# Gather operations and splits of weights ordered behind each hand-over's chain on VectorE, and a gather that pauses

## The chip, the cores and the metric

The kernel runs on one core of one Trainium2 chip, launched once. The metric is device time in microseconds: 3865.21 us, the median of three runs of the kernel before (3860.94 to 3874.12). TensorE (PE), VectorE (DVE), ScalarE (ACT), GpSimd (POOL) and SyncE (SP) run their own instruction streams in order; transfers are issued from SP's and POOL's queues.

## The reference

The input is 256 tokens of 1024 numbers, a memory and a context of 256 rows each, and a conditioning vector, all in fp32. Two blocks stand one after the other; cut to what matters:

```python
for l in range(2):                                       # first block
    x = x + 0.5 * rms_norm(swiglu(rms_norm(x, ng[0]), w_gu[l, 0], w_down[l, 0]), ng[1])   # ffn l0
    h = rms_norm(x, ng[2])
    tok, qm = retention_mixer(h, ...) if l == 0 else mla_mixer(h, ...)
    mix = concatenate([tok, memory_attention(qm, mem_n, w_kv[l])]) @ w_o[l]
    x = x + rms_norm(mix, ng[3])
    x = x + 0.5 * rms_norm(swiglu(rms_norm(x, ng[4]), w_gu[l, 1], w_down[l, 1]), ng[5])   # ffn l1
```

The second block takes that x as its latents, and a context of its own. Its scales, shifts and gates are the product of silu(c) with a large matrix (the modulation). Its even layer mixes latents and context (an mLSTM and a differential attention), its odd layer has a windowed attention; a PEER feed-forward follows each. PEER scores 128 by 128 expert keys, picks 16 experts for each of 8 heads, and computes

```python
eidx, gate = top-k picks                                  # 128 experts for each token
a = einsum('nd,nhkd->nhk', xt, u[eidx])                   # a dot product with each picked row of u
y = einsum('nhk,nhkd->nd', gate * gelu(a), v[eidx])       # a weighted sum of the picked rows of v
```

## The kernel before

Activations of 256 tokens stay in SBUF as two token tiles of 128. Weights stream in through transfers (`raw`). Every fp32 weight is split into a high part that ScalarE casts (L253, `wh`) and the rest, `wl`, that VectorE or GpSimd subtracts (L260); a product is then three matmuls (L370 to L372). Which of the two engines subtracts is counted out by a share; VectorE is the default.

Two streams are generated in turn and put in order by priority. The main one is the chain of layers: memory, ffn00, retention, ffn01, ffn10, mla, ffn11, the even layer of the latents, PEER, the odd layer, PEER. The side one computes the modulation, the context's even layer, and the context's PEER by a pick and a gather: scores and top-k (L1468 to L1600, on VectorE), and then for each of two token tiles 128 indirect transfers of rows of `u` (512 KB each, `pg`, L1636, on GpSimd) with a dot product each on VectorE (L311), and 128 of rows of `v` with a weighted sum (L1667). The rows land in a small ring of buffers: a transfer waits until the dot that read its buffer has run. These operations keep their program order among themselves ("pinned", L313).

The rest of the modulation (`mod1`) runs along with the gather: after every third pair of gather operations, once `nalong` has reached `MS`, the generator takes a step (L1614). A step issues weights on GpSimd's queue into a ring of `RN` = 4 buffers, and has TensorE multiply them (L912, `ps<-raw,cT`).

Where one layer ends and the next begins there is a hand-over: `post_add` multiplies the layer's result by its gain (L482) and takes its sum of squares; `rsqrt` computes a reciprocal root in small operations on 128 numbers (L281, L282, and three times L286 and L290); L486 adds to x; the next norm takes its sum of squares (L298 on ScalarE, L304, L306) and root in the same way and multiplies (L343, and L345 where there is a shift); TensorE transposes (L318), and L264 and L265 split the result into `xh` and `xl`. Only then can TensorE begin the next layer.

Of the kernel before, what the change touches and what calls it, by code (L numbers as in the profile page):

```python
# [8 lines left out]
F32 = mybir.dt.float32  # L9
# [157 lines left out]
class Kern:  # L167
# [3 lines left out]
    def __init__(s, ctx, tc, nc, d):  # L171
        s.ctx, s.tc, s.nc, s.d = ctx, tc, nc, d
        P = lambda n, b, **k: ctx.enter_context(tc.tile_pool(name=n, bufs=b, **k))
        s.cp = P("cst", 1)
        s.rawp = P("raw", NR)
        s.rings = {"m": (s.rawp, P("hl", NH), NR, NH, 1024, NL)}
        s.stream = "m"
        s.xtp = P("xt", 1)
        s.rp = P("res", 1)
        s.bcp = P("bc", 2)  # L180
        s.smp = P("small", 4)
        s.psp = P("ps", 1, space=PSUM)
        s.dramp = P("dram", 1, space=bass.MemoryType.DRAM)
        s.n = 0
        s.nsplit = 0
        s.share = s.base = DS
        s.cst = {}
        s.consts("base", s.cp)
        s.junk = s.cp.tile([128, 512], BF16, name="junk")
        s.ident = s.c("ident")  # L190
        s.mod, s.R = {}, {}
        s.owed = s.before = s.square = None
        s.nalong = 0

    def dq(s, out, in_):

# [51 lines left out]
    def split(s, src, n=1024):  # L248

        nc = s.nc  # L250
        ring = s.rings.get(s.stream) or s.rings["m"]
        hi = ring[1].tile([128, ring[4]], F32R, tag="wh", name=s.nm("wh"), bufs=ring[3])[:, :n]
        nc.scalar.copy(hi, src)  # L253
        s.nsplit += s.share[0]
        eng = nc.vector
        if s.nsplit >= s.share[1]:
            s.nsplit -= s.share[1]
            eng = nc.gpsimd
        lo = ring[1].tile([128, ring[4]], F32R, tag="wl", name=s.nm("wl"), bufs=ring[5])[:, :n]
        eng.tensor_tensor(lo, src, hi.bitcast(F32), op=OP.subtract)  # L260
        return hi, lo

    def split_to(s, hi, lo, src):
# [12 lines left out]
    def rsqrt(s, xh, n, tag="rs"):  # L276
# [1 line left out]
        nc = s.nc  # L278
        y = s.sm([128, n], tag + "y", I32)
        a = s.sm([128, n], tag + "a")  # L280
        nc.vector.tensor_scalar(y, xh.bitcast(I32), 1, None, op0=OP.arith_shift_right)  # L281
        nc.vector.tensor_scalar(y, y, -1.0, float(0x5F3759DF - 2 ** 31 - 2 ** 22), op0=OP.mult, op1=OP.add)  # L282
        yf = y.bitcast(F32)
        for _ in range(3):
            if n == 1:
# [23 lines left out]
    def dot(s, a, b, out):  # L309

        return s.nc.vector.scalar_tensor_tensor(a, a, 1.0, b, op0=OP.mult, op1=OP.mult, accum_out=out)  # L311

    def pin(s, i):  # L313
        return s.tc.keep_in_program_order(i) if s.pinned else i

    def tr(s, dst, src):
# [22 lines left out]
    def norm_tok(s, xn, x, mul, add, out=None):  # L339
        nc = s.nc  # L340
        halves = lambda a: [a[:, i * 512:i * 512 + 512].rearrange("p (a b) -> p a b", a=4) for i in range(2)]
        r = s.rstd(halves(x), halves(xn) if out is None else out, D)
        nc.vector.scalar_tensor_tensor(xn, x, r, mul, op0=OP.mult, op1=OP.mult)  # L343
        if add is not None:
            nc.vector.tensor_tensor(xn, xn, add, op=OP.add)  # L345

    @contextmanager
    def ahead(s, by):
# [6 lines left out]
    def norm_T(s, x, mul, add=None, kind="w", side=None, xT=None, xf=None):  # L355
        xT = xT or s.xt_tiles()
        with s.pool("np", side) as pl, s.ahead(AH):
            xn = [pl.tile([128, D], F32, tag=f"xn{t}", name=s.nm("xn")) for t in range(2)]
            rest = s.settle(xn)
            for t in range(2):  # L360
                rest(t)
                s.norm_tok(xn[t], x[:, t], mul, add)
                s.transpose_split(xn[t], xT, t, kind, xf)
        return xT


# [901 lines left out]
    def even(s, ep, x, l, v, C, kind, tk, side):  # L1268
# [4 lines left out]
        with s.pool("evo", side) as po:  # L1273
# [20 lines left out]
            with s.pool("evn", side) as pl, s.ahead(AH if lat else 0):  # L1294
# [3 lines left out]
                for t in range(2):  # L1298
# [5 lines left out]
                        s.dq(xi, x[t])  # L1304
                    s.norm_tok(xo, xi, rows[0], rows[1])
                    s.transpose_split(xo, xT, t, tk)
            with s.pool("evi", side) as pl:
                yield from s.even_in(pl, E, xT, lat, C, R, kind, tk)
            xp.close()
# [315 lines left out]
    def gather(s, hc, l, v, side, also):  # L1625
# [5 lines left out]
        with s.pool("pgg", side) as op, s.psum("psg") as pg:  # L1631
# [17 lines left out]
            for t in range(2):  # L1649
# [5 lines left out]
                for k, gt in rows(t, "u0"):  # L1655
                    s.pin(s.dot(gt, xm, A[:, k:k + 1]))
                    if k % 2:
                        yield s.gcost + s.along(also)
                nc.scalar.activation(A, A, AF.Gelu)
                nc.vector.tensor_tensor(A, A, gates[t], op=OP.mult)  # L1660
                y = pg.tile([128, D], F32, tag="pxy", name=s.nm("py"))
# [251 lines left out]
FS = (1, 1)  # L1913
FN = 2
A0 = (1, 4)
AH = 15
ME = 3
MS = 12
DB = 2
DS = (1, 4)  # L1920
OFF = dict(mod1=0, cev=0, croute=0, pick=200, gather=200)
# [58 lines left out]
```

## Time and profile before

| | |
|---|---|
| median of three runs | 3865.21 us (3860.94 to 3874.12) |
| the profiled execution | 3871.0 us |
| its span, first to last instruction | 3869.2 us |
| mean granted TensorE clock | 0.925 |
| busy: TensorE / VectorE / ScalarE / GpSimd | 3420.9 / 2706.3 / 1567.9 / 1366.4 us |
| transfers, mean over the span | 242 GB/s |

Busy times are of one execution, and shares of the whole span hide that stages have different limits; a stretch's own row tells which engine is full there. An engine's idle time is put down to what came last before the waiting instruction. The engines execute in order, so an instruction that waits holds all that stands behind it on its engine.

### The profile page before, as it was taken

How to read it: one execution, taken by the hardware profiler on the slowest of the kernel's cores; microseconds unless marked ns; L12 is line 12 of the kernel's file. 1: busy time of each engine (PE TensorE's matmuls, PEld its weight loads, DVE VectorE, ACT ScalarE, POOL GpSimd, SP SyncE). 2: the span in 40 equal slices, each digit the busy share in tenths (PEclk: the TensorE clock that was granted, in tenths of full speed). 3: DMA queues.
4: the chain of work that ended last, by engine and by line, in shares of the span. 5: the costliest groups of instructions: out<-in, count | busy, mean ns of one | idle time of the engine just before them, and what ended most of it. 6: DMA issues, size and time to landing. Idle time of an engine off the chain costs nothing.

```text
span 3869.2 us, 55141 instructions
## 1 busy us (share of the span) xinstructions
PE 3420.9 (88%) x20576; PEld 2943.2 (76%) x20576; DVE 2706.3 (70%) x5107; ACT 1567.9 (41%) x2435; POOL 1366.4 (35%) x1012
## 2 busy tenths in 40 slices
PE   5998966889899789798798799999978999899998
PEld 3776855678788578676687688889755889899987
DVE  5456788776666667787899777878976629754444
ACT  3454423343443534343213344444445115444444
POOL 3333325145445245430325366666710000122121
PEclk7999978889899889885899899999989999999999
DMA  7456549569788468761779899999941457876664
GB/s 279 145 169 216 185 161 364 185 242 327 254 314 313 169 220 298 285 232 63 255 248 387 293 339 353 352 329 341 390 126 45 142 164 248 275 243 209 196 193 150
DMA packets 316557, 938.13 MB, mean 242 GB/s; under 512 B 34608, under 2 KB 99552, under 8 KB 312192
## 3 DMA queue, kind: packets, MB, share of 16 engines
q1 hardware_dynamic: 216912, 578.25, 44.3%
q0 software_dynamic: 99376, 356.35, 25.5%
q8 instruction: 162, 2.65, 0.3%
q14 instruction: 107, 0.88, 0.1%
HBM read 894.80 MB, written 39.68 MB: 242 GB/s over the span
## 4 chain that ended last, share of the span: by engine, by line
PE 56%; DVE 17%; issue 10%; DMA 7%; POOL 7%; ACT 3%; POOLq 0%; SPq 0%; ACTq 0%; DVEq 0%
PE ps L370 14%; PE ps L371 14%; PE ps L372 14%; PE ps L417 6%; POOL pg L1636 3%; POOL wl L260 3%; DVE wl L260 2%; DVE pg L311 2%; PE ps L318 2%; DVE py L1667 1%; DMA raw<-in_modw 1%; DMA raw<-in_ffn 1%; ACT wh L253 1%; PE ps L1700 1%; DMA raw<-in_ut 1%
## 5 line engine op out<-in xcount | busy, mean ns | idle before, releaser
L253 ACT CAST wh<-raw 128x1024 fp32r<-128x1024 f32 (+3 forms) x927 | 918.6, 992 | 1062.5 <-PE ps L372 725.3
L260 DVE TENSOR_TENSOR wl<-raw,wh 128x1024 fp32r<-128x1024 f32 (+3 forms) x653 | 781.8, 1201 | 492.2 <-ACT wh L253 485.2
L260 POOL TENSOR_TENSOR wl<-raw,wh 128x1024 fp32r<-128x1024 f32 (+2 forms) x274 | 623.6, 2277 | 1397.8 <-ACT wh L253 1225.8
L370 PE MATMUL ps<-xh,wl 128*128 128x256 f32 x3008 | 872.4, 290 | 49.4 <-DVE wl L260 23.0
L371 PE MATMUL ps<-xl,wh 128*128 128x256 f32 x3008 | 864.7, 288 | 0.0
L372 PE MATMUL ps<-xh,wh 128*128 128x256 f32 x3008 | 864.4, 288 | 0.0
L370 PEld LDWEIGHTS ps<-xh,wl 128*128 128x128 f32 x3008 | 590.1, 196 | 75.7 <-DVE wl L260 26.5
L371 PEld LDWEIGHTS ps<-xl,wh 128*128 128x128 f32 x3008 | 590.2, 196 | 7.1 <-issue 2.0
L372 PEld LDWEIGHTS ps<-xh,wh 128*128 128x128 f32 x3008 | 589.5, 196 | 3.6 <-issue 3.1
L1636 POOL DMA_INDIRECT pg<-in_u,eidx x256 | 313.3, 1224 | 405.9 <-DVE pg L311 305.0
L1636 POOL DMA_INDIRECT pg<-in_v,eidx x256 | 306.5, 1197 | 398.6 <-DVE py L1667 189.6
L371 PE MATMUL ps<-wl,Wh 128*128 128x512 f32 x1024 | 403.6, 394 | 11.5 <-DVE wl L260 6.3
L370 PE MATMUL ps<-wh,Wl 128*128 128x512 f32 x1024 | 402.0, 393 | 6.5 <-DVE Wl L265 6.5
L372 PE MATMUL ps<-wh,Wh 128*128 128x512 f32 x1024 | 400.5, 391 | 0.0
L417 PE MATMUL ps<-xf,raw 128*128 128x256 f32 x1664 | 370.7, 384 | 2.3 <-ACT xf L337 2.3
L417 PEld LDWEIGHTS ps<-xf,raw 128*128 128x128 f32 x1664 | 318.4, 193 | 46.3 <-ACT xf L337 3.1
L1667 DVE SCALAR_TENSOR_TENSOR py<-pg,pA,py 128x1024 f32<-128x1024 f32 x254 | 325.9, 1283 | 7.0 <-DMA pg<-in_v,eidx 3.5
L311 DVE SCALAR_TENSOR_TENSOR pg<-pg,pxm 128x1024 f32<-128x1024 f32 x256 | 304.5, 1214 | 14.6 <-ACT pxm L1653 8.1
L371 PE MATMUL ps<-wl,xh 128*128 128x512 f32 (+4 forms) x656 | 254.0, 387 | 15.3 <-POOL wl L260 11.2
L370 PE MATMUL ps<-wh,xl 128*128 128x512 f32 (+4 forms) x656 | 247.6, 385 | 7.3 <-DVE xl L265 4.4
L372 PE MATMUL ps<-wh,xh 128*128 128x512 f32 (+4 forms) x656 | 248.5, 379 | 0.0
L371 PEld LDWEIGHTS ps<-wl,Wh 128*128 128x128 f32 x1024 | 193.8, 189 | 56.5 <-DVE wl L260 9.7
(488 smaller groups left out, 4791.7 us busy)
## 6 DMA issues: line engine op xcount, KB each, us to landing
raw<-in_ffn SPq DMA_DIRECT2D x264, 512.0 KB
raw<-in_ut SPq DMA_DIRECT2D x256, 512.0 KB
raw<-in_v SPq DMA_DIRECT2D x256, 512.0 KB
raw<-in_modw POOLq DMA_DIRECT2D x96, 512.0 KB
Gd<-Gst SPq DMA_DIRECT2D x32, 1024.0 KB
Gq<-Gd SPq DMA_DIRECT2D x30, 1024.0 KB
raw<-in_wq SPq DMA_DIRECT2D x32, 512.0 KB
raw<-in_evin POOLq DMA_DIRECT2D x24, 512.0 KB
```

Of the source, the lines that this page charges most:

```text
L253: nc.scalar.copy(hi, src)
L260: eng.tensor_tensor(lo, src, hi.bitcast(F32), op=OP.subtract)
L311: return s.nc.vector.scalar_tensor_tensor(a, a, 1.0, b, op0=OP.mult, op1=OP.mult, accum_out=out)
L318: s.nc.tensor.transpose(dst, src, s.ident[:src.shape[0], :src.shape[0]])
L370: mm(out, a[1], b[0], start=start, stop=False)
L371: mm(out, a[0], b[1], start=False, stop=False)
L372: mm(out, a[0], b[0], start=False, stop=stop)
L417: s.nc.tensor.matmul(out, src[:, k * 128:(k + 1) * 128], xf[:, k], start=(k == 0), stop=(k == 7))
L1636: nc.gpsimd.indirect_dma_start(out=got[i], out_offset=None, in_=d[tab], in_offset=bass.IndirectOffsetOnAxis(ap=eidx[t][:, k:k + 1], axis=0))
L1667: s.pin(nc.vector.scalar_tensor_tensor(y, gt, wk, y, op0=OP.mult, op1=OP.add))
L1700: nc.tensor.matmul(pb[:, t * 128:(t + 1) * 128], M[:, k, :, t0 + t], OJ[:, (t0 + t) // 2, :, t % 2], start=(k == 0), stop=(k == 1))
```

## The change

- `split`: in the main stream the first three splits (`HU`) after each hand-over put their `wl` on VectorE, whatever the share says; the second and third are ordered behind the last instruction of the norm.
- `rsqrt`: the shift and the multiply-add on the integer become one operation.
- `norm_tok`: the product with the gain (and the shift's addition) is done in two halves of 512 columns.
- `handed` and `pin`: the first pinned gather operation that is generated after a hand-over is ordered behind the last instruction of that norm. Both orderings are on the same engine and need no semaphore.
- `gather`: after the first 12 dots have been generated, the generator yields without work until three hand-overs (memory, ffn00 and retention) have been generated.
- `MS` goes from 12 to 7.

```diff
@@ split
+        hand = s.stream == "m" and s.hand
         if s.nsplit >= s.share[1]:
             s.nsplit -= s.share[1]
-            eng = nc.gpsimd
+            eng = eng if hand else nc.gpsimd
...
-        eng.tensor_tensor(lo, src, hi.bitcast(F32), op=OP.subtract)
+        i = eng.tensor_tensor(lo, src, hi.bitcast(F32), op=OP.subtract)
+        if hand:
+            if s.hand < HU:
+                s.after(i, s.last_m)
+            s.hand -= 1
@@ rsqrt
-        nc.vector.tensor_scalar(y, xh.bitcast(I32), 1, None, op0=OP.arith_shift_right)
-        nc.vector.tensor_scalar(y, y, -1.0, float(0x5F3759DF - 2 ** 31 - 2 ** 22), op0=OP.mult, op1=OP.add)
+        nc.vector.tensor_scalar(y, xh.bitcast(I32), -0.5, float(0x5F3759DF - 2 ** 31 - 2 ** 22), op0=OP.mult, op1=OP.add)
@@ new, and pin
+    def after(s, i, j):
+        s.tc.add_manual_dep(i.ins, j.ins.name, mybir.DependencyInfo(
+            mybir.DependencyClass.NoSync, mybir.DependencyReason.DATA), reason="behind the hand-over")
+    def handed(s):
+        s.held = s.last_m = s.last
+        s.hand = HU
+        s.nhands += 1
     def pin(s, i):
+        if s.held is not None:
+            s.after(i, s.held)
+            s.held = None
         return s.tc.keep_in_program_order(i) if s.pinned else i
@@ norm_tok
-        nc.vector.scalar_tensor_tensor(xn, x, r, mul, op0=OP.mult, op1=OP.mult)
-        if add is not None:
-            nc.vector.tensor_tensor(xn, xn, add, op=OP.add)
+        for i in range(2):
+            h = slice(i * 512, i * 512 + 512)
+            s.last = nc.vector.scalar_tensor_tensor(xn[:, h], x[:, h], r, mul[:, h], op0=OP.mult, op1=OP.mult)
+            if add is not None:
+                s.last = nc.vector.tensor_tensor(xn[:, h], xn[:, h], add[:, h], op=OP.add)
@@ norm_T, at its end (and in even, for the latents)
+            if s.stream == "m":
+                s.handed()
@@ gather, behind every second dot
+                    if t == 0 and k == 2 * GW - 1:
+                        while s.nhands < 3:
+                            yield None
@@ constants
+HU = 3
+GW = 6
-MS = 12
+MS = 7
```

In the after listings line numbers are shifted: L394 to L396 are L370 to L372 of before, L936 is L912, L317 is L311, L365 is L343, L272 is L265, L296 and L292 are L290 and L286, L1662 is L1636, and L200 is L198.

First place: TensorE in the tail of ffn00, where the down projection's matmuls (`ps<-wh,hh`) change over to the next unit of the up projection (`ps<-xh,wl`). Before:

```order
L371 MATMUL ps_1316<-wl_5204,hh_5019 128x512
L372 MATMUL ps_1316<-wh_5202,hh_5019 128x512
L371 MATMUL ps_1317<-wl_5204,hh_5019 128x512
L372 MATMUL ps_1317<-wh_5202,hh_5019 128x512
L912 MATMUL ps_5123<-raw_4174,cT_289 32x256
L370 MATMUL ps_5145<-xh_1242,wl_5148 128x256
L371 MATMUL ps_5145<-xl_1243,wh_5146 128x256
L372 MATMUL ps_5145<-xh_1242,wh_5146 128x256
```

The same place of TensorE in the changed order:

```order
L395 MATMUL ps_1319<-wl_5062,hh_4907 128x512
L396 MATMUL ps_1319<-wh_5060,hh_4907 128x512
L394 MATMUL ps_1316<-wh_5148,hlo_4996 128x512
L394 MATMUL ps_1317<-wh_5148,hlo_4996 128x512
L394 MATMUL ps_1318<-wh_5148,hlo_4996 128x512
L394 MATMUL ps_1319<-wh_5148,hlo_4996 128x512
L394 MATMUL ps_5091<-xh_1244,wl_5094 128x256
L395 MATMUL ps_5091<-xl_1245,wh_5092 128x256
L396 MATMUL ps_5091<-xh_1244,wh_5092 128x256
```

The matmul of the modulation (L912 on `raw_4174`) stood between the two; it now comes first in the retention.

Second place: VectorE in the hand-over from ffn00 to the retention, around the norm's product (`xn<-x,sm,bc`) of both token tiles; `pg` are the gather's dots. Before:

```order
L343 SCALAR_TENSOR_TENSOR xn_5569<-x,sm_5615,bc_5562 128x1024
L290 SCALAR_TENSOR_TENSOR sm_5648<-sm_5649,sm_5648 128x1
L311 SCALAR_TENSOR_TENSOR pg_5315,pA_4190<-pg_5315,pxm_4188 128x1024
L286 TENSOR_SCALAR sm_5649<-sm_5648,sm_5645 128x1
L311 SCALAR_TENSOR_TENSOR pg_5318,pA_4190<-pg_5318,pxm_4188 128x1024
L265 TENSOR_TENSOR xl_5565<-ps_5626,xh_5564 128x4x128
L265 TENSOR_TENSOR xl_5565<-ps_5633,xh_5564 128x4x128
L290 SCALAR_TENSOR_TENSOR sm_5648<-sm_5649,sm_5648 128x1
L311 SCALAR_TENSOR_TENSOR pg_5325,pA_4190<-pg_5325,pxm_4188 128x1024
L286 TENSOR_SCALAR sm_5649<-sm_5648,sm_5645 128x1
L311 SCALAR_TENSOR_TENSOR pg_5328,pA_4190<-pg_5328,pxm_4188 128x1024
L290 SCALAR_TENSOR_TENSOR sm_5648<-sm_5649,sm_5648 128x1
```

The same place of VectorE in the changed order, from the first product on:

```order
L365 SCALAR_TENSOR_TENSOR xn_5471<-x,sm_5515,bc_5464 128x512 x2
L292 TENSOR_SCALAR sm_5549<-sm_5548,sm_5545 128x1
L296 SCALAR_TENSOR_TENSOR sm_5548<-sm_5549,sm_5548 128x1
L292 TENSOR_SCALAR sm_5549<-sm_5548,sm_5545 128x1
L296 SCALAR_TENSOR_TENSOR sm_5548<-sm_5549,sm_5548 128x1
L365 SCALAR_TENSOR_TENSOR xn_5472<-x,sm_5548,bc_5464 128x512
L272 TENSOR_TENSOR xl_5467<-ps_5526,xh_5466 128x4x128
L272 TENSOR_TENSOR xl_5467<-ps_5533,xh_5466 128x4x128
L365 SCALAR_TENSOR_TENSOR xn_5472<-x,sm_5548,bc_5464 128x512
L263 TENSOR_TENSOR wl_5597<-raw_5589,wh_5595 128x768
L272 TENSOR_TENSOR xl_5467<-ps_5559,xh_5466 128x4x128
L272 TENSOR_TENSOR xl_5467<-ps_5566,xh_5466 128x4x128
```

The dots that stood between the norm's operations are gone from this place; the first of them stands behind the norm and five splits, and 34 more than before stand between this norm and ffn01's hand-over. The pick's last operations, which stood ahead of the dots, now stand between this hand-over's first operations, two of L1558 and two of L1559 among them.

Third place: GpSimd in the retention, `raw` the modulation's weights and `pg` the gathers. Before:

```order
L1636 DMA pg_5523<-in_u,eidx_2878 128x1024
L1636 DMA pg_5526<-in_u,eidx_2878 128x1024
L198 DMA raw_5730<-in_modw 128x1024
L1636 DMA pg_5723<-in_u,eidx_2878 128x1024
L1636 DMA pg_5726<-in_u,eidx_2878 128x1024
L198 DMA raw_5736<-in_modw 128x1024
L198 DMA modg_6181<-in_n12r 4x256
L1636 DMA pg_5819<-in_u,eidx_2878 128x1024
L1636 DMA pg_5822<-in_u,eidx_2878 128x1024
```

GpSimd in the retention in the changed order:

```order
L1662 DMA pg_5659<-in_u,eidx_2876 128x1024
L1662 DMA pg_5662<-in_u,eidx_2876 128x1024
L200 DMA raw_5684<-in_modw 128x1024
L200 DMA raw_5710<-in_modw 128x1024
L200 DMA raw_5716<-in_modw 128x1024
L1662 DMA pg_5665<-in_u,eidx_2876 128x1024
L1662 DMA pg_5668<-in_u,eidx_2876 128x1024
L1662 DMA pg_5671<-in_u,eidx_2876 128x1024
L1662 DMA pg_5674<-in_u,eidx_2876 128x1024
```

Behind `raw_5736` stand 16 gathers before the next weight in the one, and behind `raw_5716` 16 in the other. TensorE multiplies `raw_5684` to `raw_5716`, and then the two weights behind those 16 gathers and two behind another six, in one block with only a few transposes in it; in before the block has `raw_5730`, `raw_5736` and the two weights behind the gathers.

## Rows read from the trace of the kernel before

**Rows 1.** The page: busy us, share of the span and instructions.
```profile
PE 3420.9 (88%) x20576; PEld 2943.2 (76%) x20576; DVE 2706.3 (70%) x5107; ACT 1567.9 (41%) x2435; POOL 1366.4 (35%) x1012
```

**Rows 2.** What TensorE waited for in the span: us in total, times, longest.
```profile
PE ps L318 <- DVE sm L290: 79.5, 4, 30.1
PE ps L912 <- DMA raw<-in_modw: 60.6, 19, 24.6
```

**Rows 3.** Stretches: length, busy PE, PEld, DVE, ACT, POOL, PEclk, DMA share, GB/s.
```profile
500.00:631.70 131.70, 61.71 (x339) 51.16 (x338) 112.82 (x329) 29.61 (x48) 61.97 (x57) 0.71 0.70 256
631.70:791.20 159.50, 140.18 (x777) 117.98 (x775) 122.54 (x264) 66.29 (x110) 42.82 (x41) 0.89 0.69 242
...
561.00:593.10 32.10, 26.12 (x164) 21.20 (x162) 29.88 (x45) 11.94 (x17) 26.16 (x20) 1.00 0.99 376
593.10:631.70 38.60, 8.33 (x37) 7.69 (x38) 34.31 (x92) 7.89 (x20) 24.02 (x25) 0.56 0.95 355
...
631.70:687.20 55.50, 53.67 (x320) 52.02 (x318) 46.55 (x70) 28.08 (x37) 19.25 (x16) 1.00 0.97 355
687.20:711.70 24.50, 19.74 (x136) 13.72 (x136) 13.75 (x29) 8.08 (x13) 5.99 (x10) 0.86 0.58 198
711.70:791.20 79.50, 66.76 (x324) 52.25 (x323) 62.24 (x166) 30.13 (x61) 17.57 (x16) 0.83 0.53 177
```

**Rows 4.** What TensorE waited for from 500 to 631.7.
```profile
PE ps L912 <- DMA raw<-in_modw: 32.3, 3, 24.6
```

**Rows 5.** Timeline, GpSimd and TensorE: start, us, instruction, [idle before <-releaser].
```profile
529.44 0.54 POOL L198 DMA_DIRECT2D raw<-in_modw  x1 [24.51 <-DVE rd L1549]
...
533.24 1.06 PE L912 MATMUL ps<-raw,cT 128*32 128x256 f32 x2 [24.62 <-DMA raw<-in_modw]
```

**Rows 6.** VectorE by line, 593.1 to 631.7: count, busy us, mean ns, idle before.
```profile
L311 DVE SCALAR_TENSOR_TENSOR pg<-pg,pxm 128x1024 f32<-128x1024 f32 x19 | 23.0, 1211 | 3.5 <-DMA pg<-in_u,eidx 3.4
...
L486 DVE SCALAR_TENSOR_TENSOR x<-xn,sm,x 128x512 f32<-128x512 f32 x4 | 2.9, 738 | 0.0
...
L343 DVE SCALAR_TENSOR_TENSOR xn<-x,sm,bc 128x1024 f32<-128x1024 f32 x2 | 2.6, 1279 | 0.0
```

**Rows 7.** Timeline of the hand-over into ffn10, VectorE and TensorE.
```profile
1022.86 1.89 DVE L482 SCALAR_TENSOR_TENSOR xn<-ps,bc 128x512 f32<-128x512 f32 x3 [3.16 <-PE ps L372]
...
1025.32 3.17 DVE L306 SCALAR_TENSOR_TENSOR sm<-sm,sm 128x1 f32<-128x1 f32 x1
...
1035.26 0.15 DVE L306 SCALAR_TENSOR_TENSOR sm<-sm,sm 128x1 f32<-128x1 f32 x1
...
1043.08 0.55 PE L370 MATMUL ps<-xh,wl 128*128 128x256 f32 x1 [0.64 <-DVE xl L265]
```

**Rows 8.** VectorE by line and shape, 500 to 631.7: the pick.
```profile
L1559 DVE TENSOR_REDUCE cpart<-eq 128x128 f32<-128x2048 f16 x4 | 9.1, 2282 | 0.1
L1558 DVE TENSOR_TENSOR eq<-eq,SIf 128x2048 f16<-128x2048 f16 x4 | 4.9, 1220 | 0.0
```

**Rows 9.** Timeline of TensorE, then chain of waits, around the block of L912.
```profile
687.20 1.93 PE L912 MATMUL ps<-raw,cT 128*32 128x256 f32 x30
...
694.53 1.03 PE L912 MATMUL ps<-raw,cT 128*32 128x256 f32 x2 [3.52 <-DMA raw<-in_modw]
...
688.15 6.25 DMA raw<-in_modw
...
698.24 1.06 PE ps L912 x8
```

**Rows 10.** Gathers alone (L1636) on GpSimd: stretch, busy us (count), PEclk, DMA share, GB/s.
```profile
631.70:687.20 55.50, 19.25 (x16) 1.00 0.97 355
```

**Rows 11.** Timeline of GpSimd and VectorE in the hand-overs into ffn01 and ffn11.
```profile
790.29 2.37 POOL L260 TENSOR_TENSOR wl<-raw,wh 128x1024 fp32r<-128x1024 f32 x1
...
790.38 5.19 DVE L290 SCALAR_TENSOR_TENSOR sm<-sm,sm 128x1 f32<-128x1 f32 x1
...
1379.34 5.19 DVE L290 SCALAR_TENSOR_TENSOR sm<-sm,sm 128x1 f32<-128x1 f32 x1
```

More of the change, by code (lines that the diff above doesn't have):

```diff
@@ L193, in __init__ @@
         s.nalong = 0
+        s.held = s.last = s.last_m = None
+        s.hand = s.nhands = 0
     def dq(s, out, in_):
@@ L1306, in even @@
                     s.transpose_split(xo, xT, t, tk)
+                if lat:
+                    s.handed()
             with s.pool("evi", side) as pl:
```

## The prediction

> **What bounds the kernel now.** I read the page's busy shares first, then what TensorE waits for, then the stretches in which the change moves work. TensorE is busy for 3420.9 us of 3869.2 and VectorE for 2706.3 [rows 1]; what can be won is the time in which TensorE stands. Its two largest waits are transposes behind a small VectorE operation of the norm (79.5 us in four) and the modulation's matmuls, L912, behind their own weights (60.6 us in 19) [rows 2]. The reader is to see in both that the named releaser is the end of something longer: the hand-over between two layers, in which VectorE works alone, and the GpSimd queue, which holds modulation weights and gathers in one line.
>
> The stretch 500 to 631.7 has both. In its 131.7 us TensorE works 61.7 and VectorE 112.8 [rows 3]. L912 waits there for 32.3 us, 24.6 of them at once [rows 4]: GpSimd issues the weight only at 529.44, after 24.51 us of waiting for VectorE's pick (L1549, whose buffer it takes over), and TensorE, in order, stands with the rest of ffn00 behind it until 533.24 [rows 5]. Then comes the hand-over into the retention, from 593.1 to 631.1: 19 gather dots (L311), 23.0 us of VectorE, are interleaved with the norm [rows 6], and the transfer engines are 0.95 busy [rows 3]. The next stretch, the retention (631.7 to 791.2), is otherwise: TensorE works 140.2 of 159.5 us, and until 687.2 it is almost never idle, with the transfers at 0.97 [rows 3].
>
> **Term A, the stretch before the retention's norm.** Two things go. The L912 matmuls leave the tail of ffn00 (first pair of order pieces), so the 32.3 us go; I count 30, since VectorE's pick, which worked through this wait, now has splits of ffn00 in its way. And the dots leave the hand-over (second pair): all of them now stand behind the norm's last operation, where before 34 did so ahead of it. What stays is a hand-over like that of ffn10, which has no dots: from 1022.86 to 1043.08, 20.2 us, 3.0 of them the stalled L306 that is priced in term C [rows 7], so 17.2. The pick's last operations now stand in this chain: two L1558 of 1.22 and two L1559 of 2.28 [rows 8], 7.0, with four small ones some 7.7 us. That is 24.9 against 38.0, a gain of 13. A = -43 us. Bounds: if the pick only takes the place of L912 in front of ffn00's last splits, the 30 come to nothing and A is -13. If VectorE hides all of it, the stretch is TensorE's 61.7 plus about 20 of the hand-over, and A is -50. VectorE alone would need 112.8 less 35 dots of 1.21, or 70 us, so it does not forbid that. I take -43, since in the after order the pick stands between the splits and not in one block.
>
> **Term B, the retention.** The 34 dots that left A must run before ffn01's hand-over, with 34 gathers of 0.524 MB, 17.8 MB. The order shows where this hurts. TensorE reaches a block of some forty L912 after the main projection's matmuls, at 687.20 in the trace of before, and is through at 699.3 [rows 9]: 12 us, 3.5 of them a wait, since GpSimd could issue the last weights at 688.15. In after, GpSimd's queue holds weight raw_5684 behind 24 gathers (third pair). Its buffer is free only when TensorE has begun the block, for the ring has four; then come three weights, 16 gathers and two weights that TensorE needs next, then six gathers and two weights. Nothing else is ready for TensorE there. So the block lasts as long as 21 + 8 = 29 transfers of 0.524 MB. At 376 GB/s, the highest rate of these stretches (561 to 593, share 0.99) [rows 3], that is 1.39 us each and 40.4 us in all, against 12.1: +28. Their dots, 22 of 1.21, fit beside it. Ahead of the block, 18 gathers instead of 16 [rows 10] and two more weights are to move while the transfers are at 0.97 already: four times 0.524 MB at 355 GB/s, +6. Behind it are some ten more dots, 12 us of VectorE in a stretch where it works 62.2 of 79.5 [rows 3]: +1. B = +35 us.
>
> Bounds. Below: over the whole retention VectorE would work 122.5 + 34 times 1.21 = 163.7 of 159.5 us, and the idle share of the transfer engines from 687.2 to 791.2 (0.42 of 24.5 and 0.47 of 79.5, 47.7 us) would hold 17.9 MB at 376 GB/s, just what is added: B = +4. Above: from 631.7 to 687.2, sixteen gathers took 55.5 us beside the weights [rows 3, 10], 3.5 us each; 22 such gathers and seven weights of 1.4 are 87 us, B = +82. I take +35, nearest to the row of 1.39, since while TensorE stands no new layer weights are called for.
>
> The Trainium skill puts the ceiling elsewhere: "Perfetto Trace Analysis", section Roofline, says that one core is bounded by its 16 DMA engines at about 435 GB/s together. By that the 29 transfers would take an estimated 35 us, not 40, and the time would be 5 us less. The trace speaks against it: at a busy share of 0.99 the engines moved 376 GB/s [rows 3].
>
> **Term C, the other hand-overs.** The splits on GpSimd meet small VectorE operations there. At 790.38 an operation on 128 numbers takes 5.19 us while GpSimd runs a split from 790.29 [rows 11]; the same happens at 1379.34 (5.19) [rows 11] and at 1025.32 (3.17), where the same L306 takes 0.15 ten us later [rows 7]. With the three splits behind a hand-over on VectorE and two of them ordered behind the norm, these 13.1 us go. The rest is small: a reciprocal root is one operation shorter (about 0.15 us, two in each chain), and a norm's product in halves lets the transposes start after one 512-wide operation (0.74, as L486) instead of after the 1024-wide L343 (1.28) [rows 6], while the second half ends 0.2 later. I count 0.8 us in each of nine hand-overs, 7 us. The moved splits cost VectorE 1.2 us each, 27 or so, beside matmuls of which one split feeds several us; the chain of xl behind the norm may take one of them. C = -20 us, from -8 (the stalls only half gone, each hand-over longer by a split) to -28.
>
> On the halves the Trainium skill says the opposite: "VectorE: DVE Perf Modes", section Rules for kernel authors, advises fewer operations, as each pays its pipeline flush. The rows show that price (two times 0.74 against 1.28). By the rule alone the halves would lose some 0.2 us twice in each hand-over, an estimated 3.6 us, and C would be about 9 us smaller; I keep the earlier start.
>
> Elsewhere the order moves little: by ffn01's, ffn10's and ffn11's hand-overs as many dots or axpys have run in both. The added waits are without a semaphore; behind the one that is pinned to the norm stand only gather operations and splits of the same VectorE queue, and GpSimd's gathers that wait for their buffers.
>
> **Sum.** -43 + 35 - 20 = -28 us on the profiled execution's 3871.0 (its span of 3869.2 and 1.8 around it): 3843. That execution lies 5.8 above the median of 3865.2, so the forecast is 3837.
>
> **Rivals.**
> 1. The retention swallows the dots (B = +4 to +10). For it: its second part is half idle in both resources. Against it: the order puts 22 gathers where TensorE has nothing else. 3865 - 43 + 7 - 20 = 3809.
> 2. The pick takes L912's place: TensorE waits in ffn00's tail for splits behind the pick (A = -13). For it: VectorE was busy almost throughout the 24.6 us. Against it: the pick's pieces stand apart now. 3865 - 13 + 35 - 20 = 3867, no change.
> 3. Slower: the block of L912 stands behind gathers that come as slowly as beside the retention's weights. Price: 3.5 us each, B = +82, 3865 - 43 + 82 - 20 = 3884. As the block lasts 22 g + 10 us, B is 22 g + 5, and the kernel is slower by over 0.3% once a gather takes g = 3.2 us. For it: the only row of gathers beside weights has that pace. Against it: the weights' rings are full by then.
> 4. That the splits behind the hand-over still land on GpSimd, or the stalls stay: C is -8, 3849, inside the forecast's own range.
>
> **How the numbers follow.** The forecast with its own range 3815 to 3856 has a chance of 0.50 (with the fourth in it), the first rival 0.18, the second 0.17, the third 0.15. The range from 3798 to 3882 takes in most of the first and third. About 0.3%, 11.6 us, is what a measurement can tell from no change. Faster than that: 0.92 of the forecast, all of the first and a fifth of the second, 0.67. Slower: three quarters of the third and a fifth of the second, 0.15. The rest, 0.18, is the same.
>
> **What would show it.** A right: no L912 wait between 500 and the retention, no L311 before the retention's L343 has ended, some 25 us from the first L482 to the first matmul. B right: TensorE idle for 25 to 35 us on L912 in the retention, with GpSimd issuing gathers through it; that wait under 10 us is the first rival, over 70 the third. A wrong: splits (L260) as releasers of ffn00's last matmuls. C right: no operation on 128 numbers over 1 us in the hand-overs of ffn01, ffn10 and ffn11. The forecast is wrong if the retention takes under 175 or over 215 us.

## The result, and the profile after

The changed kernel takes 3821.0 us, the median of five runs (3814.5 to 3834.7), against 3865.8 for the kernel before on the same chip: a ratio of 0.9883 with a 95% interval of 0.9867 to 0.9899. That is 45 us faster; 28 were forecast, and the time lies in the stated range. The profiled execution has a span of 3819.2 us, 50.0 shorter than that of before.

The page of after, busy us and share of the span, answers to [rows 1]:

```profile
PE 3420.7 (90%) x20576; PEld 2942.4 (77%) x20576; DVE 2702.8 (71%) x5114; ACT 1567.1 (41%) x2435; POOL 1311.5 (34%) x991
```

TensorE's and VectorE's work is the same to 4 us. GpSimd has 55 us less: 253 splits in place of 274. What went is waiting. What TensorE waited for in after (us in total, times, longest), against [rows 2]:

```profile
PE ps L338 <- DVE xn L365: 57.1, 10, 18.2
PE ps L338 <- DVE xn L367: 48.6, 5, 18.8
PE ps L936 <- DMA raw<-in_modw: 31.0, 13, 6.4
...
PE ps L936 <- DVE pg L317: 18.7, 1, 18.7
```

The modulation's matmuls (L936, L912 of before) wait half as long for a transfer, and have a new wait of 18.7 us whose releaser is a gather's dot. The transposes' named releaser is now the norm's product (L365, L367), where [rows 2] names an operation on 128 numbers. That is a change of name: in before, too, the transposes of the retention start at 621.30, as the product L343 ends (621.15), and the small operation named began beside that end.

A table made from both traces tells where the 50 us went. A hand-over is counted from the first L482 (in the changed kernel L506; L945 and L969 for PEER 0, odd and PEER 1) to the first weight matmul that starts behind the norm's last product, that of the second token tile; the numbers in brackets are the gain so far.

| | before | after |
|---|---|---|
| hand-over into the retention begins | 593.1 | 554.6 (38.5) |
| its length | 35.8 | 21.1 |
| the retention's first weight matmul behind that product | 629.0 | 575.7 (53.3) |
| retention, to ffn01's hand-over | 157.9 | 198.8 |
| ffn01's hand-over begins | 786.8 | 774.5 (12.3) |
| lengths: ffn01, ffn10, mla, ffn11 | 23.9, 20.2, 18.5, 23.9 | 17.8, 16.8, 14.9, 18.2 |
| even, PEER 0, odd, PEER 1 | 30.8, 36.5, 16.4, 28.9 | 26.8, 33.5, 15.4, 28.5 |
| end | 3869.2 | 3819.2 (50.0) |

So 53 us are won ahead of the retention, 41 are given back in it, and 38 come from there to the end, 27 of them in the eight hand-overs. Where the first two are parted depends on the count, since TensorE begins the retention with the first token tile alone, in before well ahead of that product. Its first weight matmul in before and in after, and one that has the same place in the order of both, the 21st:

```profile
624.34 0.69 PE L370 MATMUL ps<-wh,xl 128*128 128x384 f32 x1 [1.10 <-DVE xl L265]
631.60 0.35 PE L372 MATMUL ps<-wh,xh 128*128 128x384 f32 x1
```

```profile
575.26 0.67 PE L394 MATMUL ps<-wh,xl 128*128 128x384 f32 x1
580.37 0.33 PE L396 MATMUL ps<-wh,xh 128*128 128x384 f32 x1
```

By the first, 49 us are won and 37 given back; by the other, which stands where the prediction's two stretches meet (631.7), 51 and 39.

**Ahead of the retention.** Two stretches that begin and end at the same work, before and then after; the columns are those of [rows 3]:

```profile
413.10:593.10 180.00, 135.44 (x929) 120.69 (x927) 143.03 (x530) 60.19 (x90) 62.88 (x62) 0.89 0.52 183
```

```profile
412.90:554.60 141.70, 126.69 (x898) 116.43 (x896) 117.92 (x489) 59.39 (x90) 33.21 (x33) 0.98 0.45 142
```

The reader is to see TensorE's busy time, the first number behind the length: it falls by 8.7 us. Of these, 4.5 are the modulation's matmuls that stood here in before and now stand in the retention:

```profile
L912 PE MATMUL ps<-raw,cT 128*32 128x256 f32 x32 | 4.5, 465 | 32.3 <-DMA raw<-in_modw 32.3
```

The other 4.3 us come from the same matmuls, 897 and 898 of them, at a granted clock of 0.98 and not 0.89. So the waits of 32.3 us, 24.6 of them at once [rows 4], had cost more than their own length.

**In the retention.** Three parts of it in after, to be laid beside the last three of [rows 3]: ahead of the block of modulation matmuls, the block, and behind it.

```profile
575.70:640.20 64.50, 59.94 (x345) 57.76 (x345) 51.46 (x77) 29.44 (x40) 26.64 (x25) 0.96 1.00 380
640.20:684.00 43.80, 11.74 (x90) 3.87 (x89) 36.62 (x65) 2.39 (x4) 29.95 (x36) 0.60 1.02 402
684.00:774.50 90.50, 78.18 (x390) 63.45 (x389) 74.30 (x187) 33.50 (x63) 21.21 (x24) 0.83 0.61 217
```

In the middle row TensorE works 11.7 of 43.8 us, VectorE 36.6, and the transfer engines are full (1.02) at 402 GB/s. The timeline of after shows the block itself; it answers to [rows 9]:

```profile
641.17 1.50 PE L936 MATMUL ps<-raw,cT 128*32 128x256 f32 x22
...
647.66 1.08 PE L936 MATMUL ps<-raw,cT 128*32 128x256 f32 x8 [3.69 <-DMA raw<-in_modw]
...
673.02 1.03 PE L936 MATMUL ps<-raw,cT 128*32 128x256 f32 x2 [18.71 <-DVE pg L317]
...
683.41 1.03 PE L936 MATMUL ps<-raw,cT 128*32 128x256 f32 x2 [6.36 <-DMA raw<-in_modw]
...
665.82 0.94 POOL L1662 DMA_INDIRECT pg<-in_u,eidx  x1 [0.30 <-issue]
...
666.75 1.16 POOL L200 DMA_DIRECT2D raw<-in_modw  x2
```

The last two rows are the sixteenth gather and, at once behind it, the two weights for which TensorE stands from 654.3 to 673.0. (The dot named as the releaser of that wait is only what ended last beside the weight's landing.) The block is through at 687.6, after 46.5 us; before it took 12.1. The whole retention, before and then after:

```profile
629.00:786.80 157.80, 137.53 (x758) 116.58 (x757) 120.22 (x257) 64.05 (x105) 40.40 (x42) 0.89 0.69 241
```

```profile
575.70:774.50 198.80, 149.86 (x822) 125.08 (x822) 162.38 (x328) 65.33 (x106) 77.81 (x84) 0.82 0.83 311
```

That is 61.8 MB for 38.0. In after 62 gathers and 16 of the modulation's weights are issued in it, in before 27 and 9: some 1.0 us was lost for each of the 42 transfers more.

### The profile page after: what moved, and what is told of

The parts are those of the page before. It is cut to its first block, busy times and chain, and to the rows that moved or that the text cites. A ratio compares the mean times of both kernels' runs of the same rounds, so it can differ in the third digit from the quotient of the medians.

```text
span 3819.2 us, 55146 instructions
## 1 busy us (share of the span) xinstructions
PE 3420.7 (90%) x20576; PEld 2942.4 (77%) x20576; DVE 2702.8 (71%) x5114; ACT 1567.1 (41%) x2435; POOL 1311.5 (34%) x991
## 4 chain that ended last, share of the span: by engine, by line
PE 58%; DVE 14%; issue 10%; DMA 8%; POOL 6%; ACT 3%; POOLq 0%; DVEq 0%; ACTq 0%; SPq 0%
PE ps L394 15%; PE ps L395 15%; PE ps L396 14%; PE ps L441 6%; POOL pg L1662 3%; POOL wl L263 3%; DVE wl L263 2%; PE ps L338 2%; DMA raw<-in_modw 2%; DVE pg L317 2%; DMA raw<-in_ffn 1%; DVE py L1696 1%; DMA pg<-in_v,eidx 1%; ACT wh L255 1%; PE ps L1729 1%
## 5 line engine op out<-in xcount | busy, mean ns | idle before, releaser
L263 DVE TENSOR_TENSOR wl<-raw,wh 128x1024 fp32r<-128x1024 f32 (+3 forms) x674 | 804.5, 1197 | 475.8 <-ACT wh L255 469.8
L263 POOL TENSOR_TENSOR wl<-raw,wh 128x1024 fp32r<-128x1024 f32 (+2 forms) x253 | 576.9, 2281 | 1395.0 <-ACT wh L255 1145.2
L394 PE MATMUL ps<-xh,wl 128*128 128x256 f32 x3008 | 870.5, 289 | 51.0 <-DVE wl L263 25.0
L396 PE MATMUL ps<-xh,wh 128*128 128x256 f32 x3008 | 862.4, 287 | 0.0
L394 PEld LDWEIGHTS ps<-xh,wl 128*128 128x128 f32 x3008 | 587.9, 195 | 78.0 <-DVE wl L263 29.5
L396 PEld LDWEIGHTS ps<-xh,wh 128*128 128x128 f32 x3008 | 587.5, 195 | 4.7 <-issue 4.4
L1662 POOL DMA_INDIRECT pg<-in_v,eidx x256 | 306.7, 1198 | 410.3 <-DVE py L1696 234.1
L1662 POOL DMA_INDIRECT pg<-in_u,eidx x256 | 304.5, 1189 | 413.7 <-DVE pg L317 331.3
L394 PE MATMUL ps<-wh,Wl 128*128 128x512 f32 x1024 | 402.5, 393 | 6.9 <-DVE Wl L272 6.9
L396 PE MATMUL ps<-wh,Wh 128*128 128x512 f32 x1024 | 401.2, 392 | 0.0
L317 DVE SCALAR_TENSOR_TENSOR pg<-pg,pxm 128x1024 f32<-128x1024 f32 x256 | 303.3, 1215 | 6.5 <-DMA pg<-in_u,eidx 5.6
L395 PE MATMUL ps<-wl,xh 128*128 128x512 f32 (+4 forms) x656 | 254.7, 388 | 21.1 <-DVE wl L263 11.9
L394 PE MATMUL ps<-wh,xl 128*128 128x512 f32 (+4 forms) x656 | 248.9, 387 | 2.3 <-DVE xl L272 1.6
L396 PE MATMUL ps<-wh,xh 128*128 128x512 f32 (+4 forms) x656 | 250.2, 382 | 0.0
```

Of the source, the lines that this page charges most:

```text
L263: i = eng.tensor_tensor(lo, src, hi.bitcast(F32), op=OP.subtract)
L394: mm(out, a[1], b[0], start=start, stop=False)
L395: mm(out, a[0], b[1], start=False, stop=False)
L396: mm(out, a[0], b[0], start=False, stop=stop)
L1662: nc.gpsimd.indirect_dma_start(out=got[i], out_offset=None, in_=d[tab], in_offset=bass.IndirectOffsetOnAxis(ap=eidx[t][:, k:k + 1], axis=0))
```

## The experiments

Each median is of four to twelve executions, against the kernel before on the same chip. Two of them (MS 34 with and without the pause) turned out to have the same order of instructions on all five engines: 3827.6 and 3820.9 us are two measurements of one program, and differences of some 7 us between medians tell nothing by themselves. Their two profiled executions lie 13.7 us apart (3826.9 and 3813.2). Where little hangs on the median, the lengths of stretches in the traces decide.

| kernel | median us | ratio to before (95%) |
|---|---|---|
| changed kernel | 3821.0 | 0.9883 (0.9867 to 0.9899) |
| without the pause, MS 12 | 3836.8 | 0.9920 (0.9906 to 0.9933) |
| before, with the pause alone | 3849.4 | 0.9951 (0.9938 to 0.9965) |
| splits shared as before | 3842.4 | 0.9930 (0.9916 to 0.9944) |
| before, with the splits alone | 3862.4 | 0.9992 (0.9974 to 1.0010) |
| norm's product in one | 3831.7 | 0.9909 (0.9894 to 0.9923) |
| gather not ordered behind the norm | 3827.1 | 0.9903 (0.9887 to 0.9919) |
| weights on SP's queue | 3821.6 | 0.9889 (0.9873 to 0.9906) |
| MS 34 | 3827.6 | 0.9893 (0.9878 to 0.9909) |
| MS 34, no pause | 3820.9 | 0.9891 (0.9875 to 0.9906) |
| gather spread | 3817.3 | 0.9859 (0.9836 to 0.9881) |
| gather spread, MS 34 | 3828.3 | 0.9889 (0.9868 to 0.9910) |

**What the pause is worth: taken out, and by itself.** Without it:

```diff
-                    if t == 0 and k == 2 * GW - 1:
-                        while s.nhands < 3:
-                            yield None
-MS = 7
+MS = 12
```

> The changed kernel without the gather's pause and with MS back at 12; the rest of the change stays. By the terms read from the two traces (before the retention's norm -50 us, retention +41, hand-overs and what follows them -41) the pause nets -9 us, so this kernel takes about 3830 us, with L912 back in ffn00's tail and dots back in the retention's hand-over. If the pause is what makes the gain (rival), it falls back to 3850 or more. If the pause only loses (its 25 us of L912 waits in the retention are not paid back), it is faster than the changed kernel, 3810 us or less.

And the pause and MS 7 put into the kernel before, with a counter of hand-overs and nothing else:

```diff
+                    if t == 0 and k == 2 * GW - 1:
+                        while s.nhands < 3:
+                            yield None
-MS = 12
+MS = 7
```

> The kernel before with the pause and MS 7 alone: splits, root, norm and the pinned order of gather operations as before. By the same terms it gains some 9 us on 3866: 3857 us, with a block of L912 in the retention that waits some 25 us. If the pause makes the gain by itself, 3825 us. If without the ordering the dots that are generated after the hand-over slip into it again, no gain ahead of the norm and 3865 or more.

3836.8 and 3849.4: the pause, with the MS that goes with it, is worth 16 us in the one (against 3821.0) and 17 in the other (against 3866.7 for before on that chip), not 9, and the rest of the change some 29. What TensorE waited for, first without the pause (414 to 810), then with it alone (412 to 790):

```profile
PE ps L338 <- DVE xn L365: 38.6, 4, 25.9
PE ps L936 <- DMA raw<-in_modw: 37.3, 4, 25.0
```

```profile
PE ps L915 <- DVE pg L312: 25.8, 3, 13.9
PE ps L319 <- DVE sm L291: 20.1, 1, 20.1
```

Without it the 25.0 us behind a weight and the long hand-over (35.8) are back; with it alone the hand-over is 20.7 and the retention 193.0 us, where before it was 157.9. Both bear out that the pause wins ahead of the norm and loses in the retention.

**The splits: taken out of the changed kernel, and put into the one before.**

```diff
-            eng = eng if hand else nc.gpsimd
+            eng = nc.gpsimd
...
-        if hand:
-            if s.hand < HU:
-                s.after(i, s.last_m)
-            s.hand -= 1
```

> The changed kernel with the splits' engine chosen as before (no VectorE preference and no ordering of splits); pause, halves, root and gather ordering stay. Stalled small VectorE operations of 3 to 5 us come back in three hand-overs: 13 us, 3834; with the shorter low-clock stretches behind them lost as well, up to 3845. The rival, that VectorE pays for the moved splits what the stalls cost, says 3821, no change.

It took 3842.4. The stall is back, as the timeline of VectorE shows in ffn01's hand-over:

```profile
787.16 5.36 DVE L292 SCALAR_TENSOR_TENSOR sm<-sm,sm 128x1 f32<-128x1 f32 x1
```

With those of 3.16 and 5.37 us in ffn10 and ffn11, the three hand-overs are 5.9, 2.3 and 5.5 us longer than in the changed kernel, 13.7 together, what term C had for the stalls. Eight more us are lost ahead of the retention's matmuls, which by the table's count begin at 584; what lost them is not shown. The kernel before with these lines added:

> The kernel before with the splits' part alone: the first three behind each hand-over on VectorE, two of them ordered behind the norm; no pause, MS 12, the norm's product, the root and the pinned gather operations as before. Taking the splits out of the changed kernel cost 21 us. If the parts add up, this one takes some 3845 us, with no small VectorE operation of 3 us or more in the hand-overs of ffn01, ffn10 and ffn11. If only the three stalls of 13.1 us go, 3853. If the splits' gain came only together with the halves or the ordering (rival), 3860 or more.

It took 3862.4, no difference. In its trace the hand-overs of ffn01, ffn10, mla and ffn11 are 18.5, 17.4, 15.6 and 19.0 us, 16.0 less in all than before, and no small operation in them takes 3 us. But the retention's matmuls begin at 637 by the table's count, 8 us later. What TensorE waited for from 410 to 640:

```profile
PE ps L931 <- DMA raw<-in_modw: 43.5, 3, 34.9
PE ps L335 <- DVE sm L297: 29.6, 1, 29.6
```

The wait behind the pick is 34.9 us here and not 24.6: in this trace it takes up part of what other places give. The time is that of the rival, a gain only together with the rest; the parts do not add up, and "the stalls go" was right while "the time falls by as much" was not.

**The norm in halves, and the gather operation ordered behind the norm.**

```diff
-        for i in range(2):
-            h = slice(i * 512, i * 512 + 512)
-            s.last = nc.vector.scalar_tensor_tensor(xn[:, h], x[:, h], r, mul[:, h], op0=OP.mult, op1=OP.mult)
-            if add is not None:
-                s.last = nc.vector.tensor_tensor(xn[:, h], xn[:, h], add[:, h], op=OP.add)
+        s.last = nc.vector.scalar_tensor_tensor(xn, x, r, mul, op0=OP.mult, op1=OP.mult)
+        if add is not None:
+            s.last = nc.vector.tensor_tensor(xn, xn, add, op=OP.add)
```

> The changed kernel with the norm's product in one 1024-wide operation again. By the earlier start of the transposes the halves are worth about 0.5 us in each of nine hand-overs: 3825. By the price of an operation more they cost some 3.6 us: 3817. Both are near what can be told; the hand-overs' own lengths in the trace decide, ffn10's of 16.8 us above all.

3831.7, slower by 11 and outside both expectations, but not where the halves were thought to work: the hand-overs of ffn01, ffn10, mla and ffn11 are 18.3, 16.7, 14.8 and 18.6 us, within half a us of the changed kernel's. Three others are longer, the retention's by 3.4, even's by 2.6 and PEER 0's by 2.8, and odd's is 1.5 shorter. In the first a third of the pick's reductions (L1583 there, 2.29 us) stands, with one more of its comparisons (1.22), in even's VectorE waits 2.4 us for a transfer where it waited 1.2, and in PEER 0's two dots of 1.21 stand between the products: the edit let other work into these places, and the 11 us are no measure of the halves. VectorE's norm in ffn10's hand-over, in the changed kernel:

```profile
1010.67 1.41 DVE L365 SCALAR_TENSOR_TENSOR xn<-x,sm,bc 128x512 f32<-128x512 f32 x2
...
1013.00 0.75 DVE L365 SCALAR_TENSOR_TENSOR xn<-x,sm,bc 128x512 f32<-128x512 f32 x1
1013.66 1.28 DVE L272 TENSOR_TENSOR xl<-ps,xh 128x512 fp32r<-128x512 f32 x2
1014.86 0.74 DVE L365 SCALAR_TENSOR_TENSOR xn<-x,sm,bc 128x512 f32<-128x512 f32 x1
```

Two halves in a row take 1.41 us where the whole took 1.28 [rows 6], and the second token tile's halves are parted by 1.28 us of other work. In a plain hand-over neither that price nor my 0.5 us shows; that an earlier start and a later end cancel is the likely reading. The rule of the Trainium skill ("VectorE: DVE Perf Modes", section Rules for kernel authors), to keep the number of operations low, agrees with the price here, 0.13 us for one operation more.

```diff
         if s.held is not None:
-            s.after(i, s.held)
             s.held = None
```

> The changed kernel with the gather operations no longer ordered behind the norm; pause, splits, root and halves stay. If the ordering does what its name says, dots and axpys of 1.2 us slip into the hand-overs of mla and even again: two to four each, 3824 to 3829. If the priorities keep them behind the chain anyway, 3821.

3827.1, near what two measurements differ by. The time lies in the range of the first expectation, but not by its mechanism: no axpy stands in mla's hand-over, which is as long as in the changed kernel, and even's has three in both; it is longer (28.5 for 26.8) by a wait for a transfer (2.6 for 1.2). The ordering of the gather operations has little to do once the splits and the pause are there.

**What holds the retention: one queue, VectorE, or the transfers.** First the weights that TensorE needs in the block, on another queue:

```diff
-        return q.dma_start(out, in_)
+        return (s.modq or q).dma_start(out, in_)    # modq: nc.sync for the weights that run along with the gather
```

> The changed kernel with the modulation's weights that run along with the gather issued on SP's queue, not behind the gathers on GpSimd's. If the block of L912 in the retention lasts 46.5 us only because its weights stand behind 22 gathers in one queue, it lasts some 15 us now and the time is 3790 to 3798. The rival, that the gathers' dots on VectorE stand right behind it (MS 34 took the block away and got 24 us in the retention, 9 of which went back in ffn01's hand-over), says a gain of at most 15 us: 3806 to 3821.

3821.6, no change, and the retention takes 201.2 us. Its stretch around the block, and what TensorE waited for from 570 to 800:

```profile
640.00:690.00 50.00, 14.94 (x91) 5.95 (x92) 36.86 (x67) 3.23 (x7) 26.36 (x29) 0.53 1.01 395
```

```profile
PE ps L939 <- DVE modo L944: 11.8, 2, 10.9
PE ps L339 <- DVE modo L942: 10.1, 1, 10.1
PE ps L939 <- DMA raw<-in_modw: 6.5, 3, 4.4
```

The weights do come sooner, and the block's last matmuls of the modulation end at 671.9, 34 us behind its first at 637.8; but then TensorE stands 10.1 us for `modo`:

```profile
669.93 1.93 PE L939 MATMUL ps<-raw,cT 128*32 128x256 f32 x16 [0.46 <-ACT qmT L642]
```

The queue alone was not it: the waits change their names, and the same 0.5 MB pieces fill the transfer engines (1.01, 395 GB/s). The new names point to VectorE, in whose order the dots stand ahead of `modo`; and VectorE, busy 36.9 of these 50 us, waits for gathers in the rest:

```profile
DVE pg L318 <- DMA pg<-in_u,eidx: 13.0, 10, 2.0
```

So the dots were made short:

```diff
-                    s.pin(s.dot(gt, xm, A[:, k:k + 1]))
+                    s.pin(s.dot(gt[:, :128], xm[:, :128], A[:, k:k + 1]))
```

> The changed kernel with each dot product on 128 of its 1024 columns (the output is not the reference's), gathers as they were. It tells VectorE from the transfers in the block of L912 (46.5 us, from 641.2 to 687.6): if the dots' time on VectorE is what lasts, the block falls to 25 us or less; if the 29 transfers are, it stays at 38 to 44.

One execution: 3793.0 us, but the retention still takes 198.1. The block, and what TensorE (592 to 783) and VectorE (640 to 686) waited for:

```profile
640.00:686.00 46.00, 13.37 (x107) 5.21 (x106) 12.78 (x66) 2.42 (x4) 31.41 (x38) 0.63 0.99 379
```

```profile
PE ps L936 <- DMA raw<-in_modw: 32.5, 5, 13.4
...
DVE pg L317 <- DMA pg<-in_u,eidx: 19.6, 18, 3.5
```

VectorE is busy 12.8 us in 46 and waits for gathers; the transfer engines are still full, and the block is as long. That the bytes hold it fits both kernels, but is not shown: none moved fewer bytes with as many gathers. A rival that no expectation named is the pace at which GpSimd issues. With short dots, as in the changed kernel, most gathers follow each other like this one:

```profile
665.72 0.94 POOL L1662 DMA_INDIRECT pg<-in_u,eidx  x1 [0.30 <-issue]
```

At 1.24 us each, the sixteen ahead of two weights take 20 us by themselves. With the weights on SP's queue that pace does not bind: there GpSimd waits some 21 of the 50 us for buffers that dots have not yet freed. Weights off the queue and short dots together, which would part the two, were not run. Of the 28 us that the kernel with short dots gains, 26 come behind the retention, in the main from ffn10's body (204.2 for 213.9) to PEER 0's hand-over (25.9 for 33.5).

**Taking the block or the gathers out of the retention.** With `MS = 34` no modulation matmul stands in ffn00's tail or in the retention.

> The changed kernel with MS 34 instead of 7: the modulation's steps begin only in ffn01, so that no L912 stands in the retention. If the block of L912 behind the gathers is what the retention lost (46.5 us where it took 12), the retention gets 25 to 35 us shorter and the time is about 3790. The rival, that the added dots and gathers bound the retention anyway, puts the wait on the transposes behind VectorE's dots and the time at 3813 to 3821.

> The changed kernel without the pause and with MS 34: dots stay in the retention's hand-over, but no L912 stands in ffn00's tail or in the retention. If L912 behind its weights was what held the tail of ffn00 (24.6 and 6.2 us), this gains some 30 us there against the kernel without the pause (3836.8): about 3805, and the pause itself is worth only the 15 us of the hand-over. The rival, that VectorE's pick holds the tail anyway, says a gain of 10 us at most: 3827 or more.

These are the two that have one order, and both times, 3827.6 and 3820.9, lie outside what either expectation gave. I had not seen that in advance: with MS 34 no dot stands before the retention's norm even without the pause. So it is not the pause alone that keeps the dots behind the norm, and at MS 34 it does nothing; why the modulation's steps draw them ahead of it at MS 12 was not settled. Of what was expected of the block half held: the retention falls to 175 us, by 24, and TensorE then waits in it for VectorE; what TensorE waited for (580 to 782), and ffn01's hand-over:

```profile
PE ps L338 <- DVE mix L813: 11.1, 1, 11.1
```

```profile
755.00:782.00 27.00, 7.17 (x30) 5.22 (x28) 26.48 (x74) 9.78 (x22) 11.11 (x11) 0.65 0.84 308
```

That hand-over has ten dots in it and takes 26.9 us, 9 more; ffn11's body, where the modulation's work now stands, takes 214.0 for 197.8. By even's first matmul, at 1589 in both (at 1581.6 in the second measurement of the one order), nothing is left that can be told.

Then a gather that does not catch up: its clock is set to the main stream's when it yields without work, and its cost is lowered so that as many operations stand before the even layer.

```diff
                 ts += (c + 0.5) / s.rate
                 continue
+            elif s.nhands:
+                ts = max(ts, tm)
...
-    s.gcost = GC[0]
+    s.gcost = GC[0] * 0.85
```

> The changed kernel, but the gather does not catch up after its pause: when it yields without work its clock is set to the main stream's, and its cost for two operations is 0.85 of what it was, so that 46 dots instead of 62 stand before ffn01's hand-over and as many as before (228 for 222) before the even layer's. If the dots in one row on VectorE make the block in the retention (the same length with the weights on another queue), 16 fewer take some 20 us off it, and the layers behind have room for them: 3797 to 3806. The rival, that each dot costs the same wherever it stands, as with MS 34, says 3815 to 3825.

> The same with MS 34, so that the retention has neither the block of L912 nor the catching up, and ffn01's hand-over has no dots in it. If the two are additive: retention near 165 us instead of 199, ffn01's hand-over 17.8: 3790 to 3800. If what is taken out of the retention comes back in ffn11 and the layers of the second half (rival): 3815 to 3825.

The first takes 3817.3, within what two measurements differ by; its interval overlaps that of the changed kernel. The trace shows why it is not 3800: the retention takes 177.6 us for 198.8, and ffn01's body is 10.4 longer and ffn10's 10.1. Its retention, to be laid beside that of after:

```profile
575.30:752.90 177.60, 147.59 (x774) 125.65 (x773) 142.38 (x292) 65.32 (x106) 62.83 (x63) 0.83 0.78 284
```

More than dots left it: 15 gathers, and with them 6 of the modulation's weights and 48 of its matmuls, 11.4 MB. So 21 transfers cost 21 us, 1.0 each, and ffn01 and ffn10, which took most of them over, paid as much; what a dot costs by itself is not parted from that. With MS 34 besides, the time is 3828.3, above both expectations: the retention is 167.9, and the bodies of ffn11 and even pay 16 and 21 us. No version beats the changed kernel by more than can be told.

## Why the prediction was right, and where its sizes were off

**Term A, -43: the mechanism held, -51 up to the end of the prediction's stretch (-53 by the table).** The modulation's matmuls left the tail, the dots left the hand-over, and the hand-over lost 14.7 us of 13 forecast. (The 38.0 us of before end behind the second token tile's transposes, at 631.1, the 20.2 of ffn10 at the first weight matmul; by the first weight matmul the retention's were 31.2, then 20.6.) The tail gave 38.5 and not 30. TensorE's idle time in it fell by 29.6 us (44.6 to 15.0), as forecast; what the sum put at nothing is 8.7 us of busy time, 4.5 for matmuls that moved into the retention and 4.3 that went with the rise of the granted clock from 0.89 to 0.98. The bound of -50 took TensorE's 61.7 us as a floor, though they hold those matmuls and their row shows a clock of 0.71 [rows 3]; the gain reached that bound. The second rival, the pick in L912's place, has one wait for it, 5.1 us behind a split at 503.6.

**Term B, +35: right in size, +39 (+41 by the table).** The block takes 46.5 us of 40.4 forecast, the part ahead of it 65.5 for 58.2 (+7 of +6), the part behind it 0.6 less (+1). The reason given was right in its size and half right in its kind: weights behind 22 gathers. On another queue they come sooner and the retention is as long, and with short dots the block is as long; the transfer engines are full, at 375 to 402 GB/s in these kernels. The bytes alone do not give the sum either: not the 17.8 MB of the 34 gathers but 23.8 MB more moved in the retention, 59 us at 402 GB/s, and part of them found idle time there (the share rose from 0.69 to 0.83). The block itself was underestimated, since more than 29 transfers moved in it (402 GB/s over 43.8 us are 33). Those 402 GB/s lie above the 376 that I had held to be the most. The ceiling of about 435 GB/s of the Trainium skill ("Perfetto Trace Analysis", section Roofline) lies above both; no stretch here reached it. The third rival had 3.5 us for a gather; in the block sixteen were issued 1.35 us apart.

**Term C, -20: undersized, -38 behind ffn01's first hand-over operation.** The three stalls were right (13.1; their hand-overs are 13.7 longer when the splits are put back). What I put at nothing: hand-overs without a long stall shrink too, mla's by 3.6 (two axpys stood in it in before) and even's and PEER 0's by 4.0 and 3.0. The 0.8 us for halves and root cannot be seen where they were expected. 11 us lie between the hand-overs; no experiment took them apart.

**The sum.** Two terms came out larger in gain and one a little larger in loss, so that 28 became 50 by the spans and 45 by the medians. What was off is the size of C above all, and behind it the busy time in A. The range held these errors because it was wide: C's 38 lies beyond its own bound of 28.

## What to carry to other kernels

Work that is moved out of an idle stretch into a full one is paid for there; here that was some 1.0 us for each 0.5 MB transfer, moved into the retention (42 for 41 us) or out of it (21 for 21 us), and neither another queue nor shorter arithmetic alone changed it. A wait's price is not its length alone: read the granted clock behind it, and do not take busy time at a low clock as a floor; but take out of the comparison the work that has moved. A hand-over's length depends on where its end is put, so put it at the same place in both traces. A small operation that takes microseconds in a hand-over is worth looking up on the engine that shares its work; but take such a part out and put it in by itself before its gain is believed, since a later wait can absorb it.

## What the hardware showed that was not expected

With gathers and the modulation's weights on GpSimd's queue, the transfer engines moved 402 GB/s over 43.8 us, more than in any stretch of before that the prediction used (376). An operation on 128 numbers takes 0.15 us, and 3.2 to 5.4 when a GpSimd split of 2.4 us or two stand beside it; with the splits on VectorE none of the three came back in any run that had them there.
